# The state-space stage of a two-block transformer kernel: rotation and scan moved into PSUM, projections one block ahead

## Chip, cores and metric

One core of a Trainium2 chip runs the whole program in one launch. The metric is the device time of the execution in microseconds, as the median of several runs; beside it stands one execution that the hardware profiler recorded.

## What is computed

512 tokens of width 1024 pass through a first block (SwiGLU, gated mixer, SwiGLU) and a second one of depth 2, whose second layer has a diagonal state-space mixer ("S5") in place of attention. Only that mixer is touched. In the reference, cut to what matters:

```python
def s5_mixer(h, a_re, a_im, log_dt, b_re, b_im, c_re, c_im, d_skip, w_glu):
    u = h.reshape(B, L, 64, 16)                  # 64 groups of 16 channels
    ...                                          # ab = exp(a * dt), bb = coef * b, complex
    bu_re = jnp.einsum('blgc,gpc->blgp', u, bb_re)
    bu_im = jnp.einsum('blgc,gpc->blgp', u, bb_im)
    _, _, x_re, x_im = lax.associative_scan(_complex_scan_op, (ar, ai, bu_re, bu_im), axis=1)
    y = einsum('blgp,gcp->blgc', x_re, c_re) - einsum('blgp,gcp->blgc', x_im, c_im)
    y = y.reshape(B, L, D) + d_skip * u.reshape(B, L, D)
    ga, gb = jnp.split(jax.nn.gelu(y) @ w_glu, 2, axis=-1)
    return ga * jax.nn.sigmoid(gb)
```

## The kernel before, in words

Activations lie channel-major: X is eight tiles of 128 channels by 512 tokens. Large products run as three passes over operands split into a high and a low half (`mm3`, L259 to L262; `gemm`, L264); `weight` (L239) loads 128 x 1024 weights on SyncE's queue into one of four `raw` buffers (L242) and splits them on ScalarE (L245) and VectorE (L246) into one of three pairs.

The stage `s5` (L1196) works on eight blocks k of 128 channels, that is eight groups each. Four successive tokens are folded together: an earlier part (`ssm_prep`) has written to DRAM, for each k, seven 128 x 512 tables: two input matrices, cos and sin of the rotation, two output matrices and the direct taps. `s5` loads them back as Rf (four tables) and Rb_ (three), L1200 to L1203, on ScalarE's DMA queue, four buffers each. With the folding a scan runs over 128 steps in each of four quarters q of a tile, and the complex recurrence is turned into a real decay `rho` between a rotation by c, s and one back.

Per block: `ahead` scales and shifts the input on VectorE (L1215) and reorders tokens on ScalarE (L1217). `gather` (L1223) brings the four token phases onto the partitions by 16 identity matmuls (L1227) of 32 output rows and copies the bank to U (L1231). `front` (L1238) projects: eight matmuls (L1247) into two banks, copied to SBUF by ScalarE (L1249). Then the rotation: six products and sums (L1255 to L1260) split between VectorE and GpSimd (`W` is VectorE for blocks 0 and 1, then GpSimd), eight scans of 128 columns (L1264), two clears (L1270, L1271) and six products and sums back (L1276 to L1281) into xr and xi, whose first column is zero so that a matmul sees the state before its step. `back` (L1284) forms the output with 48 matmuls of 32 output rows (L1292), applies GELU (L1297), splits high and low (L1299, L1300) and adds the block's share of the first two GLU products (L1305), which thus accumulate through the stage; the other 14 follow at L1318. The loop at L1307 keeps two blocks in flight between `front` and `back`.

Tiles and semaphores come from a framework that orders the instructions of each engine by program order and by a timeline that it simulates itself, so that the order on an engine can differ from that of the text; each engine then works through its list in order. The PSUM pools `pa` and `pb` have four banks each.

Of the kernel before, what the change touches and what calls it, by code (L numbers as in the profile page):

```python
# [11 lines left out]
F32 = mybir.dt.float32  # L12
# [7 lines left out]
P = 128  # L20
T = 512
# [151 lines left out]
def emit(nc, tc, A, out):  # L173
    es = ExitStack()
    with es:
# [10 lines left out]
        def nm(s):  # L186
            uid[0] += 1
            return f"{s}{uid[0]}"
# [1005 lines left out]
                yield  # L1194

        def s5(rho, acc, then):  # L1196
            with tc.tile_pool(name="sg", bufs=3, reuse_waits="tile") as sg:
                RR = []
                for k in range(KT):
                    Rf = sg.tile([P, 4, T], F32, name=nm("R"), tag="Rf", bufs=4)  # L1200
                    S.dma_start(Rf, spill[k][:, :4])
                    Rb_ = sg.tile([P, 3, T], F32, name=nm("R"), tag="Rb", bufs=4)
                    S.dma_start(Rb_, spill[k][:, 4:])  # L1203
                    RR.append((Rf, Rb_))
                Rb = spread(norm(acc.parts()))
                g, sh = GS["m", 1]
                U = [xt() for _ in range(KT)]
                hs = []

                def ahead():  # L1210
                    k = len(hs)
                    if k == KT:
                        return
                    t = tt()
                    V.scalar_tensor_tensor(t, X[k], g[:, k : k + 1], Rb, op0=ALU.mult, op1=ALU.mult)  # L1215
                    h = xt()
                    S.activation(  # L1217
                        h.rearrange("p (s j) -> p s j", s=4), t.rearrange("p (j s) -> p s j", s=4), AF.Identity,
                        bias=sh[:, k : k + 1],
                    )  # L1220
                    hs.append(h)

                def gather(k):  # L1223
                    p = psb()
                    for q in range(4):
                        for s in range(4):
                            E.matmul(  # L1227
                                p[32 * s : 32 * s + 32, q * P : (q + 1) * P], ident[:, 32 * q : 32 * q + 32],
                                hs[k][:, s * P : (s + 1) * P], start=True, stop=True, tile_position=(0, 32 * s),
                            )  # L1230
                    S.activation(U[k], p, AF.Copy)  # L1231

                GH, GL = [], []
                early = [[weight(A["glu"][j]), psa()] for j in range(2)]

                ahead()

                def front(k):  # L1238
                    gather(k)
                    ahead()  # L1240
                    R = RR[k][0]
                    z = []
                    for j in range(2):
                        p = psb()
                        for q in range(4):
                            sl = slice(q * P, (q + 1) * P)
                            E.matmul(p[:, sl], R[:, j, sl], U[k][:, sl], start=True, stop=True)  # L1247
                        t = sg.tile([P, T], F32, name=nm("z"), tag=f"z{j}")
                        S.activation(t, p, AF.Copy)  # L1249
                        z.append(t)  # L1250
                    c, s = R[:, 2, :], R[:, 3, :]
                    W = V if k < 2 else G
                    a = sg.tile([P, T], F32, name=nm("z"), tag="za")
                    b = sg.tile([P, T], F32, name=nm("z"), tag="zb")
                    V.tensor_tensor(a, z[0], c, op=ALU.mult)  # L1255
                    W.tensor_tensor(b, z[1], s, op=ALU.mult)
                    V.tensor_tensor(a, a, b, op=ALU.add)
                    (G if k < 2 else V).tensor_tensor(z[1], z[1], c, op=ALU.mult)
                    G.tensor_tensor(z[0], z[0], s, op=ALU.mult)
                    W.tensor_tensor(b, z[1], z[0], op=ALU.subtract)  # L1260
                    for t in (a, b):
                        for q in range(4):
                            sl = slice(q * P, (q + 1) * P)
                            V.tensor_tensor_scan(  # L1264
                                t[:, sl], rho[:, 4 * k + q : 4 * k + q + 1].to_broadcast([P, P]), t[:, sl], 0.0,
                                op0=ALU.mult, op1=ALU.add,
                            )
                    xr = sg.tile([P, 4, 129], F32, name=nm("xr"), tag="xr")
                    xi = sg.tile([P, 4, 129], F32, name=nm("xi"), tag="xi")
                    G.memset(xr[:, :, 0:1], 0.0)  # L1270
                    G.memset(xi[:, :, 0:1], 0.0)  # L1271

                    def v4(t):
                        return t.rearrange("p (q j) -> p q j", j=P)

                    V.tensor_tensor(z[0], a, c, op=ALU.mult)  # L1276
                    W.tensor_tensor(z[1], b, s, op=ALU.mult)
                    V.tensor_tensor(xr[:, :, 1:], v4(z[0]), v4(z[1]), op=ALU.subtract)
                    G.tensor_tensor(a, a, s, op=ALU.mult)
                    V.tensor_tensor(b, b, c, op=ALU.mult)  # L1280
                    V.tensor_tensor(xi[:, :, 1:], v4(a), v4(b), op=ALU.add)  # L1281
                    return xr, xi

                def back(k, xr, xi):  # L1284
                    R = RR[k][1]
                    p = psb()
                    for i in range(4):
                        for j in range(3):
                            for q in range(4):
                                sl = slice(q * P + 32 * i, q * P + 32 * i + 32)  # L1290
                                rhs = (xr[:, q, :P], xi[:, q, :P], U[k][:, q * P : (q + 1) * P])[j]
                                E.matmul(  # L1292
                                    p[32 * q : 32 * q + 32, i * P : (i + 1) * P], R[:, j, sl], rhs,
                                    start=j == 0, stop=j == 2, tile_position=(0, 32 * q),
                                )
                    g = tt()
                    S.activation(g, p, AF.Gelu_apprx_tanh)  # L1297
                    h, l = xt(F32R), xt(F32R)
                    S.activation(h, g, AF.Copy)  # L1299
                    V.tensor_tensor(l, g, h.bitcast(F32), op=ALU.subtract)  # L1300
                    GH.append(h)
                    GL.append(l)
                    for w, p in early:
                        sl = slice(k * P, (k + 1) * P)
                        mm3(p, w[0][:, sl], w[1][:, sl], h, l, k == 0, k == KT - 1)  # L1305

                pend = []  # L1307
                for k in range(KT):
                    pend.append((k, *front(k)))
                    if len(pend) > 2:  # L1310
                        back(*pend.pop(0))
                while pend:
                    back(*pend.pop(0))
# [42 lines left out]
```

## Time and profile before

| | |
|---|---|
| Median of 3 runs | 2458.42 us (2456.69 to 2462.13) |
| The profiled execution's own time | 2460.43 us |
| Its span, first to last instruction | 2458.3 us |
| Mean granted TensorE clock | 0.974 of full speed |
| Busy: TensorE, VectorE, ScalarE, GpSimd | 95%, 60%, 36%, 25% |

The span is what the rows below divide up; the time of an execution is 2.1 us longer here. Engine names in rows: PE is TensorE (PEld its weight loads), DVE VectorE, ACT ScalarE, POOL GpSimd, SP SyncE; a q behind a name is the engine's sequencer. "L1264" is the line of the kernel, `out<-in` the program's tile names, and brackets at a row's end tell how long the engine had stood idle and what released it. An fp32 matmul is two instructions. The ends of matmuls are modelled, so distances between starts are the safer reading.

### The profile page before, as it was taken

What the parts mean: (1) busy time and instruction counts of PE and PEld (TensorE: products, weight loads), DVE (VectorE), ACT (ScalarE), POOL (GpSimd) and SP (SyncE); (2) the same over time, 40 slices, a digit from 0 to 9 for tenths busy, and PEclk for the clock granted to TensorE, in tenths of its full rate; (3) what the DMA queues carried; (4) which work ended last, traced back from release to release, by engine and by line L of the source; (5) the groups of instructions that cost most, each with busy time, mean ns of one, the idle gap of its engine ahead of it and who ended that gap; (6) DMA issues with size and microseconds to landing.
All of it is one profiled execution on the core that took longest, in us unless ns stands there. A gap on an engine that the chain in (4) does not pass through costs nothing.

```text
span 2458.3 us, 31106 instructions
## 1 busy us (share of the span) xinstructions
PE 2338.8 (95%) x11608; PEld 1895.4 (77%) x11608; DVE 1478.2 (60%) x2748; ACT 876.1 (36%) x1374; POOL 611.5 (25%) x821
## 2 busy tenths in 40 slices
PE   8999999999999999999999989999898679999999
PEld 6888888877888888887676578787687567888887
DVE  7555565455675555446996559777644964544443
ACT  3222233533333222234345634434333222433332
POOL 2212022240122121132001313656212530111211
PEclk9999999999999999999999999999998889999999
DMA  5444445323444444331121023343425312233332
GB/s 192 157 146 154 155 137 166 106 86 114 158 156 140 155 147 154 98 101 60 52 69 61 10 86 107 97 157 129 147 91 199 121 43 95 77 95 102 95 92 79
DMA packets 94087, 281.93 MB, mean 115 GB/s; under 512 B 9841, under 2 KB 14833, under 8 KB 91889
## 3 DMA queue, kind: packets, MB, share of 16 engines
q1 hardware_dynamic: 89184, 263.30, 33.2%
q10 hardware_dynamic: 4752, 16.65, 1.9%
q8 instruction: 91, 1.49, 0.2%
q14 instruction: 60, 0.48, 0.1%
HBM read 263.14 MB, written 16.78 MB: 114 GB/s over the span
## 4 chain that ended last, share of the span: by engine, by line
PE 79%; DVE 10%; POOL 4%; issue 3%; DMA 2%; ACT 2%; SPq 0%; ACTq 0%; DVEq 0%; POOLq 0%
PE pa L260 25%; PE pa L261 24%; PE pa L262 24%; DVE wl L246 1%; DVE z L1264 1%; PE pb L950 1%; DMA raw<-in_ada 1%; PE pb L939 1%; PE pa L905 1%; ACT wh L245 1%; PE pb L314 1%; PE pb L905 1%; PE pb L319 0%; PE pa L557 0%; POOL res L1041 0%
## 5 line engine op out<-in xcount | busy, mean ns | idle before, releaser
L261 PE MATMUL pa<-x,wh 128*128 128x512 f32 x1736 | 683.8, 394 | 18.3 <-DVE x L1300 13.8
L260 PE MATMUL pa<-x,wh 128*128 128x512 f32 x1736 | 680.2, 394 | 19.4 <-ACT x L343 7.8
L245 ACT ACTIVATE wh<-raw 128x1024 fp32r<-128x1024 f32 (+2 forms) x380 | 391.9, 1035 | 836.2 <-PE pa L261 656.7
L262 PE MATMUL pa<-x,wl 128*128 128x512 f32 x1736 | 680.7, 392 | 3.2 <-DVE wl L246 3.2
L246 DVE TENSOR_TENSOR wl<-raw,wh 128x1024 fp32r<-128x1024 f32 (+2 forms) x380 | 521.9, 1376 | 249.3 <-ACT wh L245 243.5
L260 PEld LDWEIGHTS pa<-x,wh 128*128 128x128 f32 x1736 | 328.4, 190 | 93.6 <-ACT x L1299 8.2
L261 PEld LDWEIGHTS pa<-x,wh 128*128 128x128 f32 x1736 | 328.8, 189 | 93.0 <-DVE x L1300 15.8
L262 PEld LDWEIGHTS pa<-x,wl 128*128 128x128 f32 x1736 | 329.0, 190 | 72.7 <-DVE wl L246 5.1
L260 PE MATMUL pa<-u,wh 128*128 128x512 f32 x704 | 276.2, 396 | 7.1 <-ACT u L1016 7.1
L261 PE MATMUL pa<-u,wh 128*128 128x512 f32 x704 | 276.8, 394 | 1.1 <-POOL u L1017 1.1
L262 PE MATMUL pa<-u,wl 128*128 128x512 f32 x704 | 275.0, 394 | 2.4 <-DVE wl L246 2.4
L368 DVE SCALAR_TENSOR_TENSOR ada<-raw,c,ada 128x512 f32<-128x512 f32 x168 | 129.5, 771 | 220.2 <-DMA raw<-in_ada 219.1
L402 POOL TENSOR_TENSOR t<-t,t 128x512 f32<-128x512 f32 x44 | 72.3, 1643 | 496.2 <-DVE t L401 286.5
L1013 POOL TENSOR_TENSOR t<-t,t 128x512 f32<-128x512 f32 x44 | 58.8, 1336 | 429.5 <-ACT t L1012 423.0
L260 PE MATMUL pa<-wh,x 128*128 128x512 f32 (+1 forms) x384 | 151.1, 401 | 14.4 <-DVE t L805 6.1
L260 PEld LDWEIGHTS pa<-u,wh 128*128 128x128 f32 x704 | 133.2, 189 | 39.2 <-ACT u L1016 8.4
L262 PEld LDWEIGHTS pa<-u,wl 128*128 128x128 f32 x704 | 133.6, 190 | 32.6 <-DVE wl L246 4.1
L261 PEld LDWEIGHTS pa<-u,wh 128*128 128x128 f32 x704 | 133.9, 190 | 30.5 <-POOL u L1017 1.9
L262 PE MATMUL pa<-wh,x 128*128 128x512 f32 (+1 forms) x384 | 150.6, 394 | 0.0
L261 PE MATMUL pa<-wl,x 128*128 128x512 f32 (+1 forms) x384 | 149.7, 390 | 0.0
L288 POOL TENSOR_TENSOR acc<-acc,t 128x512 f32<-128x512 f32 x45 | 73.0, 1628 | 174.2 <-ACT t L282 164.1
L260 PEld LDWEIGHTS pa<-wh,x 128*128 128x128 f32 x384 | 85.2, 223 | 31.9 <-issue 10.4
(360 smaller groups left out, 2885.6 us busy)
## 6 DMA issues: line engine op xcount, KB each, us to landing
raw<-in_ada SPq DMA_DIRECT2D x96, 512.0 KB, 3.9
raw<-in_u SPq DMA_DIRECT2D x88, 512.0 KB, 3.6
raw<-in_f1u SPq DMA_DIRECT2D x44, 512.0 KB, 3.7
raw<-in_f2u SPq DMA_DIRECT2D x44, 512.0 KB, 3.5
raw<-in_d SPq DMA_DIRECT2D x32, 512.0 KB, 3.5
raw<-in_aq SPq DMA_DIRECT2D x28, 512.0 KB, 3.8
dr<-res SPq DMA_DIRECT2D x8, 1536.0 KB, 7.6
raw<-in_wpg SPq DMA_DIRECT2D x20, 512.0 KB, 3.6
```

Of the source, the lines that this page charges most:

```text
L245: S.activation(h[:, :w], r[:, :w], AF.Copy)
L246: eng.tensor_tensor(l[:, :w], r[:, :w], h[:, :w].bitcast(F32), op=ALU.subtract)
L260: E.matmul(ps, ah, bh, start=first, stop=False)
L261: E.matmul(ps, ah, bl, start=False, stop=False)
L262: E.matmul(ps, al, bh, start=False, stop=last)
L288: G.tensor_tensor(self.sums[0], self.sums[0], sq, op=ALU.add)
L314: E.matmul(p[:, 8 * j + o + b : 8 * j + o + b + 1], a[:, tokens(b, by4)], ones, start=True, stop=True)
L368: V.scalar_tensor_tensor(acc, r[:, j * T : (j + 1) * T], kk, acc, op0=ALU.mult, op1=ALU.add)
L402: G.tensor_tensor(b, a, b, op=ALU.mult)
L905: E.matmul(ps[e][:, :W], QT[pr][base : base + 64, n * P : (n + 1) * P], KTT[pr][base : base + 64, :W], start=True, stop=True,)
L939: E.transpose(p[:, j * P : (j + 1) * P], s[:, j * P : (j + 1) * P], ident)
L1013: G.tensor_tensor(b, a, b, op=ALU.mult)
```

## The change

All of it lies in `s5`. What it does:

- The scaled input of blocks 1 to 7 is formed on GpSimd from an SBUF copy of the norm's factors; block 0 reads them from PSUM on VectorE. The gain moves into ScalarE's reordering instruction.
- The gather writes into the first of the block's two projection banks; the projection then overwrites that bank.
- `project` runs one block ahead of `front`: gather, copy to u, projection of the imaginary part first. It also has ScalarE spread rho over 512 columns (`rt`, column 0 of each quarter zero), so that one scan of 512 columns restarts at each quarter.
- The products, sums and scans of the rotation are done by VectorE in place in the two banks. For the way back ScalarE copies one part to SBUF and VectorE and GpSimd share the work; the last block has VectorE alone.
- xr, xi and rt live in fixed buffers, used alternately, whose zero columns are cleared once.
- The output product is 12 full-width matmuls over one bank; GELU follows, and a second gather (`blocks`) brings the result into channel order.
- One block rather than two is kept in flight; R of blocks 3 to 7 is loaded on SyncE's queue, Rb_ has three buffers.

The new text of the changed functions (what they replace is printed above):

```diff
...
                 for k in range(KT):
+                    q = S if k < 3 else nc.sync
                     Rf = sg.tile([P, 4, T], F32, name=nm("R"), tag="Rf", bufs=4)
+                    q.dma_start(Rf, spill[k][:, :4])
+                    Rb_ = sg.tile([P, 3, T], F32, name=nm("R"), tag="Rb", bufs=3)
+                    q.dma_start(Rb_, spill[k][:, 4:])
...
+                for t in (*xri, *rt):
+                    G.memset(t[:, :, 0:1], 0.0)
+                rp = spread(norm(acc.parts()))
+                Rb = kept(rp)
...
+                def blocks(p, src):
                     for q in range(4):
                         for s in range(4):
                             E.matmul(
                                 p[32 * s : 32 * s + 32, q * P : (q + 1) * P], ident[:, 32 * q : 32 * q + 32],
+                                src[:, s * P : (s + 1) * P], start=True, stop=True, tile_position=(0, 32 * s),
                             )
+                    return p
+
+                def ahead():
...
+                    if k == 0:
+                        V.tensor_tensor(t, X[k], rp, op=ALU.mult)
+                    else:
+                        G.tensor_tensor(t, X[k], Rb, op=ALU.mult)
+                    h = tt()
+                    S.activation(
+                        h.rearrange("p (s j) -> p s j", s=4), t.rearrange("p (j s) -> p s j", s=4), AF.Identity,
+                        bias=sh[:, k : k + 1], scale=g[:, k : k + 1],
+                    )
...
+                def project():
...
                     ahead()
+                    z = [psb(), psb()]
+                    u = sg.tile([P, T], F32, name=nm("U"), tag="U", bufs=4)
+                    S.activation(u, blocks(z[0], H[k]), AF.Copy)
...
+                    for j in (1, 0):
                         for q in range(4):
                             sl = slice(q * P, (q + 1) * P)
+                            E.matmul(z[j][:, sl], R[:, j, sl], u[:, sl], start=True, stop=True)
+                    S.activation(
+                        rt[k % 2][:, :, 1:], rho[:, 4 * k : 4 * k + 4].unsqueeze(2).to_broadcast([P, 4, 127]), AF.Copy
+                    )
...
+                def front(k):
+                    project()
+                    zr, zi = pre[k]
...
+                    d, a = st("z"), st("z")
+                    V.tensor_tensor(d, zi, c, op=ALU.mult)
+                    V.tensor_tensor(zi, zi, s, op=ALU.mult)
+                    V.tensor_tensor(a, zr, c, op=ALU.mult)
+                    V.tensor_tensor(zi, zi, a, op=ALU.add)
+                    V.tensor_tensor(zr, zr, s, op=ALU.mult)
+                    V.tensor_tensor(zr, d, zr, op=ALU.subtract)
+                    rk = rt[k % 2].rearrange("p q j -> p (q j)")
+                    for t in (zr, zi):
+                        V.tensor_tensor_scan(t, rk, t, 0.0, op0=ALU.mult, op1=ALU.add)
+                    wr, wi = zi, zr
...
+                    if k < KT - 1:
+                        S.activation(m[1], wi, AF.Copy)
+                        V.tensor_tensor(m[0], wr, c, op=ALU.mult)
+                        V.tensor_tensor(m[2], wr, s, op=ALU.mult)
+                        G.tensor_tensor(m[3], m[1], c, op=ALU.mult)
+                        G.tensor_tensor(xi[:, :, 1:], v4(m[2]), v4(m[3]), op=ALU.add)
+                        G.tensor_tensor(m[1], m[1], s, op=ALU.mult)
+                        G.tensor_tensor(xr[:, :, 1:], v4(m[0]), v4(m[1]), op=ALU.subtract)
+                    else:
...
+                def back(k, xr, xi):
+                    R = RR[k][1]
+                    p = psa()
+                    for j in (2, 1, 0):
                         for q in range(4):
                             sl = slice(q * P, (q + 1) * P)
+                            rhs = (xr[:, q, :P], xi[:, q, :P], U[k][:, sl])[j]
+                            E.matmul(p[:, sl], R[:, j, sl], rhs, start=j == 2 and q == 0, stop=j == 0 and q == 3)
+                    y = tt()
+                    S.activation(y, p, AF.Gelu_apprx_tanh)
+                    p = blocks(psa(), y)
                     h, l = xt(F32R), xt(F32R)
+                    S.activation(h, p, AF.Copy)
+                    V.tensor_tensor(l, p, h.bitcast(F32), op=ALU.subtract)
...
                     pend.append((k, *front(k)))
-                    if len(pend) > 2:
+                    if len(pend) > 1:
                         back(*pend.pop(0))
```

## Rows read from the trace of the kernel before

**Rows 1.** The page, part 1: busy time, share of the span, instructions.
```profile
PE 2338.8 (95%) x11608; PEld 1895.4 (77%) x11608; DVE 1478.2 (60%) x2748; ACT 876.1 (36%) x1374; POOL 611.5 (25%) x821
```

**Rows 2.** Busy time by stretch; columns: us, engines' busy us (instructions), clock, DMA.
```profile
1883.31:1898.44 15.13, 9.73 (x77) 8.83 (x77) 6.66 (x19) 5.02 (x6) 0.00 (x0) 0.57 0.99 394
1898.44:1952.03 53.59, 35.01 (x535) 29.52 (x534) 48.31 (x72) 16.47 (x24) 30.27 (x22) 0.80 0.43 153
1952.03:1965.22 13.19, 10.38 (x165) 8.36 (x164) 12.95 (x18) 4.80 (x8) 7.47 (x7) 1.00 0.32 107
```

**Rows 3.** Timeline of VectorE, one block; columns: start, duration, engine, line, operation.
```profile
1965.22 3.66 DVE L1264 TENSOR_TENSOR_SCAN z<-c,z 128x128 f32<-128x128 f32 x8
...
1971.07 1.77 DVE L1278 TENSOR_TENSOR xr<-z,z 128x512 f32<-128x512 f32 x1
1972.76 1.75 DVE L1280 TENSOR_TENSOR z<-z,R 128x512 f32<-128x512 f32 x1
...
1976.04 1.80 DVE L1257 TENSOR_TENSOR z<-z,z 128x512 f32<-128x512 f32 x1
...
1978.37 3.66 DVE L1264 TENSOR_TENSOR_SCAN z<-c,z 128x128 f32<-128x128 f32 x8
```

**Rows 4.** Timeline of GpSimd in that block.
```profile
1970.56 1.73 POOL L1279 TENSOR_TENSOR z<-z,R 128x512 f32<-128x512 f32 x1
1972.44 1.52 POOL L1256 TENSOR_TENSOR z<-z,R 128x512 f32<-128x512 f32 x1 [0.16 <-ACT z L1249]
```

**Rows 5.** Timeline of VectorE elsewhere, first operand in PSUM.
```profile
1143.33 0.68 DVE L804 TENSOR_TENSOR t<-pa,sm 128x512 f32<-128x512 f32 x1
1143.93 0.68 DVE L805 TENSOR_TENSOR t<-pa,sm 128x512 f32<-128x512 f32 x1
```

**Rows 6.** Timeline of all engines elsewhere: VectorE from PSUM beside GpSimd.
```profile
38.12 0.68 DVE L399 TENSOR_TENSOR t<-pa,rb 128x512 f32<-128x512 f32 x1
...
38.35 1.29 POOL L402 TENSOR_TENSOR t<-t,t 128x512 f32<-128x512 f32 x1 [16.97 <-ACT t L400]
```

**Rows 7.** Timeline of VectorE in block 0: an add, its four scans, what follows.
```profile
1904.04 0.66 DVE L1260 TENSOR_TENSOR z<-z,z 128x512 f32<-128x512 f32 x1
1904.74 1.37 DVE L1264 TENSOR_TENSOR_SCAN z<-c,z 128x128 f32<-128x128 f32 x4
1906.03 0.67 DVE L1276 TENSOR_TENSOR z<-z,R 128x512 f32<-128x512 f32 x1
```

**Rows 8.** VectorE groups by line and shape: busy us, mean ns.
```profile
L956 DVE TENSOR_TENSOR x<-pb,x 128x128 fp32r<-128x128 f32 x16 | 4.5, 281 | 10.8 <-ACT x L955 10.7
```

**Rows 9.** Timeline of TensorE, first blocks; x counts merged instructions.
```profile
1895.69 3.63 PE L1247 MATMUL pb<-x,R 128*128 128x128 f32 x16 [0.72 <-ACT x L1231]
...
1903.03 1.08 PE L1227 MATMUL pb<-x,c 128*32 128x128 f32 x32
1904.83 2.05 PE L1247 MATMUL pb<-x,R 128*128 128x128 f32 x16 [0.72 <-ACT x L1231]
...
1909.76 1.96 PE L1227 MATMUL pb<-x,c 128*32 128x128 f32 x32
```

**Rows 10.** Timeline of TensorE at the stage's end.
```profile
2008.33 0.95 PE L260 MATMUL pa<-x,wh 128*128 128x512 f32 x3 [0.71 <-ACT x L1299]
...
2009.39 0.40 PE L262 MATMUL pa<-x,wl 128*128 128x512 f32 x1
...
2010.31 0.39 PE L262 MATMUL pa<-x,wl 128*128 128x512 f32 x1
```

**Rows 11.** Timeline of ScalarE; ACTq is its queue issuing a DMA.
```profile
1891.78 1.21 ACT L1217 ACTIVATE x<-t,c 128x512 f32<-128x512 f32 x1 [6.96 <-DVE t L1215]
...
1912.43 0.60 ACT L1249 ACTIVATE z<-pb 128x512 f32<-128x512 f32 x1 [5.81 <-POOL z L1279]
```

**Rows 12.** Waits on SyncE's queue: who for whom, us, times, longest.
```profile
SPq L242 <- DVE wl L246: 98.6, 2, 94.8
```

**Rows 13.** DMA issues in the stage: count, KB each, us to landing.
```profile
R<-dr ACTq DMA_DIRECT2D x8, 1024.0 KB, 5.4
```

More of the change, by code (lines that the diff above doesn't have):

```diff
@@ L1233, in s5 @@
                 GH, GL = [], []
                 early = [[weight(A["glu"][j]), psa()] for j in range(2)]
-                ahead()
-                def front(k):
-                    gather(k)
+                pre = []
+                def project():
+                    k = len(U)
+                    if k == KT:
+                        return
                     ahead()
+                    z = [psb(), psb()]
+                    u = sg.tile([P, T], F32, name=nm("U"), tag="U", bufs=4)
+                    S.activation(u, blocks(z[0], H[k]), AF.Copy)
+                    U.append(u)
@@ L1251, in front @@
-                    c, s = R[:, 2, :], R[:, 3, :]
[L1252 to L1279, printed above, removed]
@@ L1280, in front, with v4 @@
-                    V.tensor_tensor(b, b, c, op=ALU.mult)
-                    V.tensor_tensor(xi[:, :, 1:], v4(a), v4(b), op=ALU.add)
+                            E.matmul(z[j][:, sl], R[:, j, sl], u[:, sl], start=True, stop=True)
+                    S.activation(
+                        rt[k % 2][:, :, 1:], rho[:, 4 * k : 4 * k + 4].unsqueeze(2).to_broadcast([P, 4, 127]), AF.Copy
+                    )
+                    pre.append(z)
+                ahead()
+                project()
+                def v4(t):
+                    return t.rearrange("p (q j) -> p q j", j=P)
@@ new lines, in front, with st @@
+                def front(k):
+                    project()
+                    zr, zi = pre[k]
+                    R = RR[k][0]
+                    c, s = R[:, 2, :], R[:, 3, :]
+                    def st(n):
+                        return sg.tile([P, T], F32, name=nm("z"), tag=n, bufs=3 if n == "z" else 2)
+                    d, a = st("z"), st("z")
[9 more added lines that the diff above has]
+                    wr, wi = zi, zr
+                    xr, xi = xri[2 * (k % 2)], xri[2 * (k % 2) + 1]
+                    m = [st(f"m{j}") for j in range(4)]
+                    if k < KT - 1:
[7 more added lines that the diff above has]
+                    else:
+                        V.tensor_tensor(m[3], wi, c, op=ALU.mult)
+                        V.tensor_tensor(m[1], wi, s, op=ALU.mult)
+                        V.tensor_tensor(wi, wr, s, op=ALU.mult)
+                        V.tensor_tensor(xi[:, :, 1:], v4(wi), v4(m[3]), op=ALU.add)
+                        V.tensor_tensor(wr, wr, c, op=ALU.mult)
+                        V.tensor_tensor(xr[:, :, 1:], v4(wr), v4(m[1]), op=ALU.subtract)
@@ L1285, in back @@
                     R = RR[k][1]
[L1286 to L1297, printed above, removed]
+                    p = psa()
+                    for j in (2, 1, 0):
+                        for q in range(4):
+                            sl = slice(q * P, (q + 1) * P)
+                            rhs = (xr[:, q, :P], xi[:, q, :P], U[k][:, sl])[j]
[3 more added lines that the diff above has]
+                    p = blocks(psa(), y)
                     h, l = xt(F32R), xt(F32R)
-                    S.activation(h, g, AF.Copy)
-                    V.tensor_tensor(l, g, h.bitcast(F32), op=ALU.subtract)
+                    S.activation(h, p, AF.Copy)
+                    V.tensor_tensor(l, p, h.bitcast(F32), op=ALU.subtract)
                     GH.append(h)
```

39 lines of the change are left out of this document (9 added, 30 removed).

## The prediction, made before the changed kernel was run

> **What bounds the kernel now.** I read the page's part 1 first: TensorE is busy for 95% of the span [rows 1], so over the whole kernel little can move. Its table of slices shows the exceptions, and the state-space stage is the longest of them, so I cut the span by stretch. From the last down-projection (1883.31 us) the stage has 15.1 us of start, in which TensorE has work for 9.7 us and the granted clock averages 0.57. From the first rotation product (1898.44) on, VectorE is busy 48.3 of 53.6 us, and later 12.95 of 13.19 us in one whole block of 128 channels, at clock 1.00 and with TensorE busy 10.4 us by modelled ends [rows 2]. Here VectorE sets the pace, not TensorE. The end of the stage is the last matmul of the two early GLU accumulations, 2010.31 + 0.39 = 2010.70 us [rows 10]; behind it TensorE is full again.
>
> VectorE's timeline of one block says why a block takes 13.15 us (the distance between the two rows of scans): eight scans take 3.6 us, and three two-operand instructions last 1.75 to 1.80 us [rows 3] where the same kind lasts 0.66 or 0.67 alone [rows 7]. GpSimd is reading SBUF in those moments [rows 4]. So some 3.3 us of the block are VectorE held while GpSimd runs, and one more is in the scans: four of them alone take 1906.03 - 1904.74 = 1.29 us, 0.32 each, or 2.6 for eight [rows 7].
>
> **The change part by part.**
>
> *Rotation and scan in PSUM.* The two copies of z by ScalarE go, and VectorE works in place on the projection's banks: six products and sums, two scans, then two products out (the last block: six), and the subtraction that splits off the low half, which now also reads PSUM. That is nine 512-column instructions and two scans per block; GpSimd keeps five. A VectorE instruction with one operand in PSUM starts every 0.60 us and lasts 0.68 [rows 5], no more than one fed from SBUF [rows 7]. And one that ran beside GpSimd kept its 0.68 us while GpSimd kept 1.29 [rows 6]. All of VectorE's steady work in the new stage has at most one operand in SBUF, so I take the holding of [rows 3] as gone. Nine by 0.60 is 5.4 us.
> [...]
> No row shows VectorE writing PSUM. Below 0.60 it cannot go, since the reading end alone sets that start distance; above, I bound it by each of the six writers taking its stream twice: four more 0.60 and two more scans, 4.6 us per block. I take 0.60, since rows 5 is the nearest, and keep the other end as a rival.
>
> *512-column scans.* No row has one. A scan of 128 columns lasts about 0.39 us (1.37 less three distances of 0.32 is 0.41, [rows 7]), a product of 128 columns 0.281 [rows 8] and one of 512 columns 0.68, so 384 columns more cost 0.40 at the product's rate, and 0.80 at twice that. From 0.32 that is 0.72 to 1.12 us each. The scan's extra 0.11 to 0.13 us at 128 columns fits the doubled rate (0.13 by the same slope), so I take 1.12, 2.24 for both. A dependent instruction starts about 0.70 after its source rather than 0.60 [rows 7]; four such places add 0.4.
> VectorE per block: 5.4 + 2.24 + 0.4 = 8.0 us (7.2 with the cheap scan), against 13.15.
>
> *Gather in the projection's bank, block-diagonal output at full width, second gather.* Per block TensorE issues a gather (32 instructions, 1.08 us), the projection (16 in 2.05) [rows 9], the output product as 12 full-width matmuls, 24 instructions, 3.1 us at the projection's pace, in place of 96 narrow ones, a second gather, 1.08, and six early matmuls at 0.23, 1.4 [rows 10]: 8.7 us. At the half clock, by the other rows of the same lines (1.96 and 3.63 us [rows 9]), it is 1.96 + 3.63 + 5.4 + 1.96 + 2.8 = 15.8. So TensorE comes level with VectorE and is late next. Its queue is in order, and three results come back through ScalarE in each block: the gathered u, the GELU and the high half. One such wait is 0.72 us [rows 9]; if none is filled with other work, 8.7 + 2.2 = 10.9 us per block.
>
> *Input scaling moved to GpSimd (blocks 1 to 7).* GpSimd: five instructions by 1.29 [rows 6], 6.5 us, under both. The 128-row zero columns are cleared once rather than per block; they cost nothing on a GpSimd with this slack. If the slack went, 0.1 us each.
>
> *ScalarE.* Out: two z copies. In: one m copy, one decay table, a u copy and GELU and high half as before. 1.21 + five by 0.60 [rows 11] is 4.2 us, 4.8 if the broadcast table costs as much as the strided 1.21. Hidden under 8 us. The Rb copy of the norm lies beside the first scaled input, which now reads the bank itself.
>
> *Loads of R for blocks 3 to 7 moved to SyncE's queue.* On ScalarE's queue a load that waited for its buffer held ScalarE for 5.81 us [rows 11]; that goes. On SyncE's queue they stand among the GLU weight loads, one of which waited 94.8 us for a buffer [rows 12]. Ten loads, each behind its own freed buffer: a 1 MB load lands 5.4 us after issue [rows 13], against a block of 8 to 9 us and a projection a block ahead, so I cost it at nothing; with three rather than four Rb buffers the load of block k+3 waits for the output product of block k, and Rf of the next stands behind it. If that cover failed, each block would wait up to 5.4 us.
>
> *One block less in flight, projections a block ahead.* The z banks come in pairs of four, so projection k+2 waits for rotation k. It then needs 1.08 + 0.72 + 2.05 = 3.9 us, and rotation k+1 lasts 8, which covers it.
>
> **The sum.** Rotation 0 can begin when the first half of the projection is done, 1895.69 + 1.8 = 1897.5 us [rows 9]. Two blocks without an output product at 8.0, six at 9.5 (between VectorE's 8.0 and TensorE's unfilled 10.9) make 73 us. The last block has four more products on VectorE, 2.4. Behind them: last eight matmul instructions 1.0, GELU 0.7, gather 1.1, high half 0.7, low half 0.7, last early matmuls 0.9, so 5.1, and 2 for a part of it at half clock. 1897.5 + 73 + 2.4 + 5.1 + 2 = 1980.0 against 2010.7: 30.7 us saved. The profiled execution took 2460.43 us with a span of 2458.3, 2.0 above the median of the runs; 2460.4 - 30.7 = 2429.7, and from the median 2458.4, **2427.7 us**. About 0.2% (5 us) is what a measurement of this kernel can tell from no change.
>
> **The rivals.**
> - *VectorE alone sets the pace.* With TensorE's waits all filled a block takes 7.2 to 8.0 us. Eight blocks are 58 to 64, and 9 to 15 us more are saved than in the sum: 2412 to 2419 us. For it: the order before already slips gathers between output products (1903.03, with no idle time shown [rows 9]). Against it: 8.7 us of TensorE work per block. Chance 0.15.
> - *Writing PSUM costs a second stream*, or waits pile up. A block takes up to 8.0 + 4.6 = 12.6 us; eight are 101, and about 3 us are saved at the far end, 2455 us; halfway 2441. No row speaks against it; rows 5 speak for the reading end alone. Chance 0.15, a fifth of it within 0.2%.
> - *The holding stays.* If products fed from PSUM are also held by GpSimd, five GpSimd instructions hold VectorE 1.1 us each and a block takes 13.5: no change, 2458 us. Rows 6 speak against it. Chance 0.03.
> - *Slower: TensorE at half clock.* The place is blocks 1 to 7: each hand-over leaves TensorE idle, the clock falls, and the 15.8 us of a block then exceed the 13.15 it has now. From 1893.7 us (the first projection less its gather, [rows 9]) eight blocks by 15.8 and a tail of 7, the 5.1 with its TensorE part doubled, end near 2027, 16 us late: 2475. It decides once more than about two thirds of a block's TensorE work runs at half clock (8.7 to 15.8 passes 13.15). For it: clock 0.57 at the start and 0.80 in the next stretch [rows 2]. Against it: 1.00 in a block whose pace VectorE set, so with more idle time for TensorE than the new one leaves [rows 2]. [...] Chance 0.07.
>
> **How the numbers follow.** The forecast itself, 8.0 to 10.9 us per block in steady state, has 0.60: from 2418 (six blocks 1.5 faster) to 2437. Faster takes forecast, the first rival and four fifths of the second: 0.87 and a little of the half-clock case where it holds only part of the stage, 0.89. Within 0.2%: the held case and a fifth of the second, 0.05. Slower 0.06. The range drops the ends of the first rival and the last two: 2414 to 2446.
>
> **What would show each step.** Right: VectorE's products at 0.68 us with GpSimd busy beside them, GpSimd at 1.26 to 1.29 throughout, scans near 1.2 us, rotations 8 to 10 us apart, the last early matmul near 1980. Wrong: in-place products above 0.8 us (second rival); products of 1.7 us (the holding); projection rows of 3.6 us in blocks 3 to 7 with clock near 0.5 (half clock); VectorE waiting for TensorE more than 2 us a block (TensorE's waits dearer than 10.9); TensorE's projection waiting for a DMA (SyncE's queue).

## The result, and the profile after

| | before | after |
|---|---|---|
| Median, on the same chip | 2460.28 us | 2430.38 us (2426.51 to 2431.24) |
| Ratio | 1 | 0.9877 [0.9861, 0.9894] |
| The profiled execution's own time | 2460.43 us | 2431.24 us |
| Its span | 2458.3 us | 2429.5 us |

(A fourth execution took 4470.66 us, for a reason not looked into; it is in the median of the right column but not in the ratio or the bounds.) The change makes the kernel 1.2% faster, 2.7 us above the forecast of 2427.7 and inside its range. The first part of the page, to be read beside [rows 1], follows; line numbers from here on are those of the changed kernel.

```profile
PE 2338.0 (96%) x11288; PEld 1900.8 (78%) x11288; DVE 1449.9 (60%) x2701; ACT 875.9 (36%) x1374; POOL 599.4 (25%) x810
```

To see the stage alone I measure it between two instructions that every version has: VectorE's first step on the norm's statistics (L334) and its first weight split behind the stage (L246), in "stage" below. Before it ran from 1886.35 to 2010.68 us, 124.3; after from 1888.65 to 1981.42, 92.8. So 31.6 us went out of it. Of that 2.3 are missing in the span because the stage begins later in this execution (its start lay between 1880.9 and 1888.7 us over the versions below, whose code ahead of the stage is the same; what sets it was not tried), and 0.5 behind it: 31.6 - 2.3 - 0.5 = 28.8.

VectorE's timeline of one block, during which GpSimd worked without a gap (beside [rows 3]):

```profile
1923.36 0.69 DVE L1279 TENSOR_TENSOR z<-pb,R 128x512 f32<-128x512 f32 x1
1923.96 0.69 DVE L1280 TENSOR_TENSOR pb<-pb,R 128x512 f32<-128x512 f32 x1
1924.56 0.68 DVE L1281 TENSOR_TENSOR z<-pb,R 128x512 f32<-128x512 f32 x1
1925.16 0.69 DVE L1283 TENSOR_TENSOR pb<-pb,R 128x512 f32<-128x512 f32 x1
1925.76 0.69 DVE L1282 TENSOR_TENSOR pb<-pb,z 128x512 f32<-128x512 f32 x1
1926.36 0.69 DVE L1284 TENSOR_TENSOR pb<-z,pb 128x512 f32<-128x512 f32 x1
1926.95 2.33 DVE L1287 TENSOR_TENSOR_SCAN pb<-rt,pb 128x512 f32<-128x512 f32 x2
1929.19 0.67 DVE L1293 TENSOR_TENSOR z<-pb,R 128x512 f32<-128x512 f32 x1
1929.78 0.67 DVE L1294 TENSOR_TENSOR z<-pb,R 128x512 f32<-128x512 f32 x1
1930.38 0.68 DVE L1279 TENSOR_TENSOR z<-pb,R 128x512 f32<-128x512 f32 x1
```

GpSimd's timeline in it (beside [rows 4]):

```profile
1925.31 1.28 POOL L1296 TENSOR_TENSOR xri<-z,z 128x512 f32<-128x512 f32 x1
1926.54 1.28 POOL L1297 TENSOR_TENSOR z<-z,R 128x512 f32<-128x512 f32 x1
1927.78 1.27 POOL L1232 TENSOR_TENSOR t<-x,rb 128x512 f32<-128x512 f32 x1
```

Every product and sum on VectorE, those that write PSUM in place too, lasts 0.67 to 0.69 us, and the next instruction starts 0.60 us after it; GpSimd keeps 1.28. Two scans take 1929.19 - 1926.95 = 2.24 us. This block lasts 7.02 us; with the subtraction of a low half, which falls between blocks here, 7.6, against 13.15 before.

Busy time by stretch (columns as in [rows 2]), cut at the first products of blocks 0, 3, 4, 5, 6 and 7, at block 7's way back and at the stage's end:

```profile
1886.00:1900.97 14.97, 8.64 (x74) 7.74 (x74) 4.61 (x16) 8.62 (x10) 3.88 (x5) 0.67 1.01 413
1900.97:1923.36 22.39, 18.02 (x212) 15.67 (x212) 21.84 (x32) 8.75 (x13) 10.61 (x9) 0.84 0.40 144
1923.36:1930.38 7.02, 7.02 (x96) 6.41 (x98) 7.02 (x11) 2.20 (x4) 7.02 (x7) 1.00 0.47 168
1930.38:1941.98 11.60, 11.60 (x150) 9.94 (x141) 8.37 (x13) 5.73 (x9) 10.31 (x9) 1.00 0.75 292
1941.98:1950.23 8.25, 8.25 (x115) 7.67 (x114) 7.72 (x12) 4.01 (x6) 3.13 (x3) 1.00 0.29 97
1950.23:1959.00 8.77, 8.16 (x110) 7.13 (x110) 7.75 (x12) 2.67 (x5) 6.17 (x6) 1.00 0.27 92
1959.00:1966.32 7.32, 7.32 (x86) 6.29 (x88) 6.63 (x9) 1.19 (x2) 3.00 (x3) 1.00 0.01 2
1966.32:1981.43 15.11, 13.40 (x120) 10.66 (x112) 5.07 (x9) 2.89 (x5) 0.00 (x0) 1.00 0.00 1
```

VectorE sets the pace up to 1923 (21.84 of 22.39 us). From block 3 on TensorE has nearly no gap (one of 0.6 us up to 1959), while VectorE has some after its full block 3: blocks 3 to 6 take 1959.00 - 1923.36 = 35.64 us, 8.9 each, where VectorE needs 7.6. Its waits, from the groups by line (1898 to 1985 us; busy, mean ns, then idle time before them by releaser):

```profile
L1279 DVE TENSOR_TENSOR z<-pb,R 128x512 f32<-128x512 f32 x8 | 5.5, 685 | 8.5 <-PE pb L1257 8.4
L1281 DVE TENSOR_TENSOR z<-pb,R 128x512 f32<-128x512 f32 x8 | 5.5, 682 | 1.6 <-PE pb L1257 1.6
L1321 DVE TENSOR_TENSOR x<-pa,x 128x512 fp32r<-128x512 f32 x8 | 5.5, 682 | 6.6 <-ACT x L1320 6.6
```

Most of this lies at the two ends: 6.4 us of L1279's wait stand ahead of block 0, and 4.4 of L1321's in the tail. Within blocks 3 to 6 VectorE waits 4.8 us in all, 2.5 for the projection and 2.3 for a high half.

### The profile page after: what moved, and what is told of

Its sections match the earlier page's. It is cut to its first block, busy times and chain, and to the rows that moved or that the text cites. A ratio compares the mean times of both kernels' runs of the same rounds, so it can differ in the third digit from the quotient of the medians.

```text
span 2429.5 us, 30407 instructions
## 1 busy us (share of the span) xinstructions
PE 2338.0 (96%) x11288; PEld 1900.8 (78%) x11288; DVE 1449.9 (60%) x2701; ACT 875.9 (36%) x1374; POOL 599.4 (25%) x810
## 4 chain that ended last, share of the span: by engine, by line
PE 77%; DVE 10%; POOL 4%; issue 4%; DMA 3%; ACT 2%; ACTq 0%; SPq 0%; DVEq 0%; POOLq 0%
PE pa L260 24%; PE pa L262 23%; PE pa L261 23%; DMA raw<-in_ada 2%; DVE wl L246 2%; PE pb L950 1%; PE pb L314 1%; PE pb L939 1%; ACT wh L245 1%; DVE x L723 1%; PE pa L905 1%; PE pb L905 1%; PE pb L1257 1%; POOL t L1013 0%; POOL res L1041 0%
## 5 line engine op out<-in xcount | busy, mean ns | idle before, releaser
L246 DVE TENSOR_TENSOR wl<-raw,wh 128x1024 fp32r<-128x1024 f32 (+2 forms) x380 | 520.9, 1373 | 259.7 <-ACT wh L245 249.7
L262 PEld LDWEIGHTS pa<-u,wl 128*128 128x128 f32 x704 | 132.9, 189 | 31.4 <-DVE wl L246 3.0
L260 PEld LDWEIGHTS pa<-wh,x 128*128 128x128 f32 x384 | 85.5, 223 | 31.4 <-issue 10.4
```

The lines of the kernel that those rows point to most:

```text
L246: eng.tensor_tensor(l[:, :w], r[:, :w], h[:, :w].bitcast(F32), op=ALU.subtract)
L260: E.matmul(ps, ah, bh, start=first, stop=False)
L262: E.matmul(ps, al, bh, start=False, stop=last)
```

## The experiments

All ten work on the changed kernel. Diffs are against it; where a version builds on another experiment, the text says so.

| version | median us | ratio to before | stage us |
|---|---|---|---|
| before | 2458 to 2460 | 1 | 124.3 |
| changed | 2430.38 | 0.9877 [0.9861, 0.9894] | 92.8 |
| e_sbuf | 2459.5 | 1.0005 [0.9994, 1.0017] | 124.0 |
| e_vec | 2442.39 | 0.9936 [0.9919, 0.9953] | 108.0 |
| e_sbufvec | 2443.86 | 0.9943 [0.9928, 0.9958] | 110.4 |
| e_scan128 | 2431.03 | 0.9895 [0.9877, 0.9913] | 93.5 |
| e_dve2 | 2431.83 | 0.9901 [0.9884, 0.9917] | 98.2 |
| e_narrow | 2419.52 | 0.9853 [0.9836, 0.9871] | 86.4 |
| e_nargather | 2434.31 | 0.9902 [0.9886, 0.9919] | 96.5 |
| e_gelu | 2420.78 | 0.9842 [0.9828, 0.9857] | 85.8 |
| e_best2 | 2425.0 | 0.9862 [0.9846, 0.9877] | 89.3 |
| e_actq | 2427.86 | 0.9879 [0.9863, 0.9896] | 93.2 |

The ratios also carry the start of the stage, which shifts from one execution to the next; the stage column does not, but it is one execution each, so how far it scatters is not known.

**e_sbuf: rotation and scan in SBUF again.**

```diff
-                    zr, zi = pre[k]
+                    zs = []
+                    for j in range(2):
+                        t = xt()
+                        S.activation(t, pre[k][j], AF.Copy)
+                        zs.append(t)
+                    zr, zi = zs
```

> The changed kernel, but ScalarE copies both projection banks to SBUF and the rotation and the scans work there. Theory (a VectorE instruction with one operand in PSUM is not held while GpSimd reads): with both operands in SBUF again, products that meet a GpSimd instruction last 1.7 to 1.8 us instead of 0.68; some four or five of them per block add 4 to 5 us to VectorE's 7.5, a block goes from 8.9 to 11.5 to 13 us and the time to 2447 to 2460 us. Rival (the gain is from the 512-column scans, the projections ahead and one kind of output matmul): VectorE stays below TensorE's 8.9 us a block, the copies are hidden on ScalarE, 2430 us within 5.

The whole gain is gone: ratio 1.0005, stage 124.0 us, at the slow end of the theory's range. Groups by line of this kernel (1898 to 2000 us), three of VectorE and one of GpSimd:

```profile
L1284 DVE TENSOR_TENSOR z<-x,R 128x512 f32<-128x512 f32 x8 | 10.3, 1292 | 10.6 <-ACT x L1274 10.6
L1285 DVE TENSOR_TENSOR x<-x,R 128x512 f32<-128x512 f32 x8 | 9.8, 1221 | 0.0
L1326 DVE TENSOR_TENSOR x<-pa,x 128x512 fp32r<-128x512 f32 x7 | 4.8, 688 | 15.2 <-ACT x L1325 15.2
```

```profile
L1300 POOL TENSOR_TENSOR z<-z,R 128x512 f32<-128x512 f32 x7 | 14.8, 2111 | 44.1 <-ACT z L1297 44.1
```

The same products that last 685 and 690 ns from PSUM now average 1292 and 1221, and GpSimd is held in turn (2111 instead of 1280). L1326, the one with an operand in PSUM, keeps its 688. Over the six lines of products with R VectorE is busy 47.9 us against 31.4 in the changed kernel, 16.5 of the 31.2 us lost. But VectorE also waits for ScalarE, 25.8 us in the rows of L1284 and L1326 (9.2 of them ahead of block 0), and TensorE's mean granted clock from the first product of block 2 to that of block 6 is 0.87 against 0.96. So this run alone could not tell the holding, with what queues behind it, from the extra pass through ScalarE. The next two do.

**e_vec and e_sbufvec: the same pair without GpSimd.** e_vec puts GpSimd's five instructions of a block on VectorE, which also makes ScalarE's copy for the way back needless; e_sbufvec has in addition the copies of e_sbuf.

```diff
-                        G.tensor_tensor(t, X[k], Rb, op=ALU.mult)
+                        V.tensor_tensor(t, X[k], Rb, op=ALU.mult)
...
-                        S.activation(m[1], wi, AF.Copy)
-                        V.tensor_tensor(m[0], wr, c, op=ALU.mult)
-                        V.tensor_tensor(m[2], wr, s, op=ALU.mult)
-                        G.tensor_tensor(m[3], m[1], c, op=ALU.mult)
-                        G.tensor_tensor(xi[:, :, 1:], v4(m[2]), v4(m[3]), op=ALU.add)
-                        G.tensor_tensor(m[1], m[1], s, op=ALU.mult)
-                        G.tensor_tensor(xr[:, :, 1:], v4(m[0]), v4(m[1]), op=ALU.subtract)
+                        V.tensor_tensor(m[3], wi, c, op=ALU.mult)
+                        V.tensor_tensor(m[1], wi, s, op=ALU.mult)
+                        V.tensor_tensor(m[2], wr, s, op=ALU.mult)
+                        V.tensor_tensor(m[0], wr, c, op=ALU.mult)
+                        V.tensor_tensor(xi[:, :, 1:], v4(m[2]), v4(m[3]), op=ALU.add)
+                        V.tensor_tensor(xr[:, :, 1:], v4(m[0]), v4(m[1]), op=ALU.subtract)
```

> The changed kernel with all element-wise work of the stage on VectorE: GpSimd's scaled input and its four products and sums of the way back move there (five instructions by 0.60 us), the ScalarE copy in front of them goes. Everything else as changed, rotation in PSUM. VectorE's block grows from 7.2 to 10.2 us, past the 8.9 us that TensorE sets now, so about 1.3 us in each of seven blocks: near 2440 us (2436 to 2446). It is the control for the next kernel: no GpSimd work beside VectorE in either.

> The same, and in addition ScalarE copies both projection banks to SBUF and VectorE rotates and scans there, as in the SBUF experiment that lost the whole gain (2459.5 us). Theory A, the gain was lost because GpSimd holds VectorE when both read SBUF: without GpSimd work nothing holds it, products last 0.67 us, and it is as fast as its control, within 5 us (2440 to 2446), so faster than with GpSimd's help. Theory B, the gain was lost through the extra pass through ScalarE (two copies of 0.6 us between projection and rotation, and behind other ScalarE work): it stays 20 to 30 us behind its control, 2460 to 2470 us, with VectorE waiting for ScalarE for several us in each block.

2442.39 us, as expected, and 2443.86: with GpSimd out of the way, going back to SBUF costs 2.4 us of stage; with GpSimd at work it costs 31.2. The 2.4 us lie at the start: the first product comes 16.4 us after the statistics instead of 13.6, and between there and the tail VectorE never waits for ScalarE. Theory A holds, B falls (with the reservation that VectorE is full in both of these, so that the pair does not show what the longer way through ScalarE costs where VectorE has slack). The products in SBUF, groups by line of e_sbufvec, last what they last in PSUM, for which one line of e_vec follows:

```profile
L1285 DVE TENSOR_TENSOR x<-x,R 128x512 f32<-128x512 f32 x8 | 5.6, 699 | 0.0
L1284 DVE TENSOR_TENSOR z<-x,R 128x512 f32<-128x512 f32 x8 | 5.6, 697 | 8.3 <-ACT x L1274 8.3
```

```profile
L1280 DVE TENSOR_TENSOR pb<-pb,R 128x512 f32<-128x512 f32 x8 | 5.6, 696 | 0.0
```

So GpSimd's help is worth 15 us of stage with the rotation in PSUM (108.0 to 92.8), and costs 14 with it in SBUF (110.4 to 124.0). Both kinds of source stand side by side in e_sbuf: 1221 ns with two operands in SBUF (L1285), 688 with one in PSUM (L1326).

**e_scan128: eight 128-column scans in place of two of 512,** still in PSUM.

```diff
-                        V.tensor_tensor_scan(t, rk, t, 0.0, op0=ALU.mult, op1=ALU.add)
+                        for q in range(4):
+                            sl = slice(q * P, (q + 1) * P)
+                            V.tensor_tensor_scan(
+                                t[:, sl], rho[:, 4 * k + q : 4 * k + q + 1].to_broadcast([P, P]), t[:, sl], 0.0,
+                                op0=ALU.mult, op1=ALU.add,
+                            )
```

> The changed kernel with eight scans of 128 columns per block again, in PSUM, in place of two of 512. Theory (TensorE, busy without a gap from the fourth block on, sets the pace at 8.9 us a block, and the long scan only runs at the half rate that its 1.13 us shows): VectorE gets 8 x 0.32 - 2 x 1.13 = 0.3 us more per block and stays under TensorE: 2430 us within 4. Rival (the long scans are a main part of the gain): eight start-ups more on the path of each block, 1 us or more per block, 2438 us or more.

2431.03 us, stage 93.5: no difference that can be told. The long scans are no measurable part of the gain. The projections a block ahead and the smaller moves were not taken back one by one; e_sbuf, which keeps them, has no gain left.

**e_dve2: 1.2 us more VectorE work per block,** one product formed three times.

```diff
+                    V.tensor_tensor(a, zr, c, op=ALU.mult)
+                    V.tensor_tensor(a, zr, c, op=ALU.mult)
                     V.tensor_tensor(zi, zi, a, op=ALU.add)
```

> The changed kernel with one product per block (zr by c) done three times over: 1.2 us more on VectorE per block, 9.6 us in all, same result. Theory (TensorE is the bound from the fourth block on, VectorE in the first three and in the last): VectorE goes from 7.2-7.8 to 8.4-9.0 us, about level with TensorE's 8.9; 3 to 6 us slower, 2433 to 2436 us. Rival (VectorE still sets the pace in all blocks): the whole 9.6 us, 2440 us.

1.5 us in the median, 5.4 in the stage, of 9.6 us added; by the ratios it is 6 us, but their intervals overlap. The stage is as the theory had it, the median below its 3 to 6 us. The place tells which engine leads where. From L334 to the first product of block 3 it is 1924.85 - 1887.20 = 37.65 us against 34.71, 2.9 of the 3.6 us added there; from block 3 to block 7 it is 1962.25 - 1924.85 = 37.40 against 35.64, 1.8 of 4.8. So VectorE leads at first and later has slack: 3.0 of the 4.8 us vanish in four blocks, about 0.8 a block.

**e_narrow and e_nargather: TensorE's work.** e_narrow forms the output directly in channel order by narrow matmuls, u's part first, so that the second gather goes (1.06 to 1.08 us of TensorE per block). e_nargather, whose diff (the second) is against e_narrow, puts that gather back as dead work.

```diff
                     for j in (2, 1, 0):
-                        for q in range(4):
-                            sl = slice(q * P, (q + 1) * P)
-                            rhs = (xr[:, q, :P], xi[:, q, :P], U[k][:, sl])[j]
-                            E.matmul(p[:, sl], R[:, j, sl], rhs, start=j == 2 and q == 0, stop=j == 0 and q == 3)
+                        for i in range(4):
+                            for q in range(4):
+                                sl = slice(q * P + 32 * i, q * P + 32 * i + 32)
+                                rhs = (xr[:, q, :P], xi[:, q, :P], U[k][:, q * P : (q + 1) * P])[j]
+                                E.matmul(
+                                    p[32 * q : 32 * q + 32, i * P : (i + 1) * P], R[:, j, sl], rhs,
+                                    start=j == 2 and i == 0, stop=j == 0 and i == 3, tile_position=(0, 32 * q),
+                                )
                     y = tt()
                     S.activation(y, p, AF.Gelu_apprx_tanh)
-                    p = blocks(psa(), y)
                     h, l = xt(F32R), xt(F32R)
-                    S.activation(h, p, AF.Copy)
-                    V.tensor_tensor(l, p, h.bitcast(F32), op=ALU.subtract)
+                    S.activation(h, y, AF.Copy)
+                    V.tensor_tensor(l, y, h.bitcast(F32), op=ALU.subtract)
```

```diff
                     S.activation(y, p, AF.Gelu_apprx_tanh)
+                    blocks(psa(), y)
                     h, l = xt(F32R), xt(F32R)
```

> The changed kernel with the output product in 48 matmuls of 32 output rows again (U's part still first), which need no second gather. Theory (TensorE sets the pace from the fourth block on): a block has 96 narrow instructions, 2.6 us at full clock, in place of 24 wide ones and a gather, 4.1 us; TensorE falls from 8.7 to 7.2 us a block, VectorE's 7.5 to 8 takes over, the tail loses a gather and a wait: 5 to 10 us faster, 2420 to 2425 us. Rival (VectorE or the waits between the engines already set the pace): within 3 us of 2430, or slower by the narrow matmuls at half clock.

> The narrow-output experiment (2419.5 us; 86.4 us from the norm's statistics to the first weight split behind the stage, against 92.8 in the changed kernel) with the second gather put back as dead work: 32 narrow matmuls of the GELU's result into a PSUM bank that nobody reads, 1.08 us of TensorE per block. Theory A, the changed kernel is paced by TensorE's sum of work: TensorE has 7.5 us of work in a 7.6 us block of the narrow version, so 1.1 us more makes a block 8.6 us and gives back most of the gain: 91 to 94 us of stage, 2425 to 2429. Theory B, the chain through the second gather (gather, then high half, then early products) is what costs, not the work: the dead gather is filled in, and the stage stays within 2 us of 86.4, the time at 2418 to 2421.

e_narrow takes 6.4 us out of the stage, and its 2419.52 us lie just below the range of the theory. So the full-width output with its second gather is a part of the change that cost time. From block 3 to block 7 VectorE is now full in every block, 31.17 of 31.17 us; TensorE has no gap in the first two of these four and gaps of 0.15 and 0.92 us in the others (the third block, then the sum of the four, columns as above):

```profile
1938.33:1945.94 7.61, 7.46 (x150) 6.16 (x142) 7.61 (x13) 4.15 (x7) 6.84 (x6) 1.00 0.43 147
sum 31.17, PE 30.11 PEld 25.43 DVE 31.17 ACT 14.69 POOL 25.09; mean PE 7.53 PEld 6.36 DVE 7.79 ACT 3.67 POOL 6.27
```

The dead gather alone gives all of that back and 3.7 us more. (The ratios of e_narrow and of the changed kernel overlap, as do those of the changed kernel and e_nargather; the times themselves, each version on another chip, do not: 2419.03 to 2424.17 us, 2426.51 to 2431.24 without the 4470.66, and 2432.40 to 2437.64.) That its result is used by nobody excludes the chain behind it (theory B); its place behind the GELU in TensorE's list remains. The sum of work (A) has the direction but not the size, 10.1 us of stage where 8 x 1.08 = 8.6 were added. The timeline of e_nargather, all engines, shows one place where more than the work is lost:

```profile
1933.15 0.63 ACT L1324 ACTIVATE x<-t 128x512 fp32r<-128x512 f32 x1
...
1934.03 2.33 DVE L1287 TENSOR_TENSOR_SCAN pb<-rt,pb 128x512 f32<-128x512 f32 x2
...
1937.45 1.48 DVE L1325 TENSOR_TENSOR x<-t,x 128x512 fp32r<-128x512 f32 x1
...
1938.99 0.50 PE L261 MATMUL pa<-x,wh 128*128 128x512 f32 x1 [2.87 <-DVE x L1325]
...
1940.04 1.95 PE L1257 MATMUL pb<-U,R 128*128 128x128 f32 x16
...
1941.13 0.69 DVE L1279 TENSOR_TENSOR z<-pb,R 128x512 f32<-128x512 f32 x1 [2.20 <-PE pb L1257]
```

The high half is ready at 1933.78, but VectorE's list has scans and products ahead of the subtraction for the low half (L1325), which starts at 1937.45 and, with both inputs in SBUF and GpSimd at work beside it, lasts 1.48 us (672 ns on average in e_gelu below, with one input in PSUM). TensorE, in order, waits 2.87 us for it with the next projection (L1257) standing behind; and VectorE then waits 2.20 us for that projection. The same comes once more, ahead of block 7: TensorE waits 0.69 us for a low half at 1957.24, and VectorE 1.75 for the projection behind it at 1958.94. In e_narrow TensorE waits for a low half twice, 1.7 us in all, but VectorE for no projection after block 0's. So two lists in order, each waiting for the other, can cost more than the added work; how the 10.1 us divide was not tried.

**e_gelu and e_best2: two more edits on e_narrow.** e_gelu is e_narrow with GELU in place in PSUM (`y = p` for `y = tt()`), so that the low half reads one operand from PSUM. e_best2 has in addition the norm's copy behind block 0's scaled input.

```diff
-                Rb = kept(rp)
...
                 ahead()
+                Rb = kept(rp)
                 project()
```

> The narrow-output experiment with GELU in place in its PSUM bank alone (without moving the norm's copy): the low half's subtraction then has one operand in PSUM and always lasts 0.69 us. In the narrow version it was held twice, by 0.96 and 0.69 us. VectorE sets the pace there: 1 to 2 us less of stage, 84.5 to 85.5 us, 2417 to 2420. If the order of work shifts as in the version with both edits, 87 to 90 us of stage.

> The narrow-output experiment (2419.5 us) with two edits more: the copy of the norm's factors goes behind block 0's scaled input, which had waited for it (about 0.7 us at the start), and GELU writes in place to its PSUM bank, so that the subtraction for the low half has one operand in PSUM and isn't held by GpSimd (it lasted 1.4 to 1.6 us at times, up to 0.9 us in some of eight blocks). If VectorE sets the pace there, as its trace without gaps says, 2 to 6 us less: 2414 to 2418. If TensorE's order of work sets it after all, only the first 0.7 us: 2419.

e_gelu: the low half's mean falls from 886 to 672 ns, the stage from 86.4 to 85.8 us, less than the 1 to 2 us expected, and its ratio 0.9842 [0.9828, 0.9857] lies clear of the changed kernel's; against e_narrow's it can't be told apart. These two are the fastest measured. e_best2 missed: 2425.0 us, not 2414 to 2418 or 2419. The scaled input does start 0.6 us sooner after the statistics, but ScalarE's list then has another reordering ahead of the copy of u, as its timeline shows:

```profile
1896.37 1.30 ACT L1233 ACTIVATE t<-t,c,c 128x512 f32<-128x512 f32 x1 [1.39 <-POOL t L1231]
1897.57 0.58 ACT L1250 ACTIVATE U<-pb 128x512 f32<-128x512 f32 x1
```

The first rotation product comes 12.5 us after the statistics (1900.31 - 1887.78), in e_narrow 12.4, and VectorE waits for two later projections, 1.03 and 0.93 us. These are 2 of the 3.5 us of stage by which it lies behind e_gelu; the rest was not traced.

**e_actq: all loads of R on ScalarE's queue.**

```diff
-                    q = S if k < 3 else nc.sync
+                    q = S
```

> The changed kernel with all R loads on ScalarE's queue, as before the change. Theory: a load that waits for its buffer (the five loads of Rb waited 29 us for the output product on SyncE's queue) holds ScalarE, which now feeds TensorE three times a block; some of it shows, 2434 to 2445 us, with ScalarE idle several us behind TensorE or VectorE at the loads. Rival: the buffers come free before ScalarE gets there, so the queue makes no difference: within 3 us of the changed kernel's 2430.

2427.86 us, stage 93.2: the rival was right, the queue makes no difference.

## Why the prediction was right, and where its sum was off

**What bounds.** Right, as far as was tried: VectorE, held by GpSimd, set the pace before. The two pairs show, in the changed kernel, that the place in PSUM pays because it ends the holding: 31.2 - 2.4 = 29 us of stage, 16.5 of them in the products themselves and the rest in what queues behind, which the pairs do not divide. The kernel before was not run without GpSimd's share.

**The rotation in PSUM.** "I take 0.60" and "the holding of [rows 3] as gone" both held: nine instructions 0.60 us apart, 0.67 to 0.69 long, beside a GpSimd at 1.28. The bound of a second stream for writing PSUM (4.6 us a block) fell; its rival goes with it. A PSUM source cost no more than an SBUF one: the same six products and sums last 697 to 700 ns from SBUF in e_sbufvec and 690 to 701 from PSUM in e_vec.

**The scans.** 1.12 us each was what they take: 2.24 for two, where products of the same width start 0.60 apart.

**VectorE per block.** The sum said 8.0; it is 7.6. The step that failed is "four such places add 0.4": the order on VectorE has L1283 ahead of L1282, so that most instructions find their source done, and the rest are 0.60 apart too.

**TensorE comes level and is late next.** Right, from block 3 on; the first rival, VectorE alone, holds only up to there. The six blocks "at 9.5 (between VectorE's 8.0 and TensorE's unfilled 10.9)" were too dear, 8.9 in the four measured; the waits for ScalarE are filled by other work. From the first product to the last sum (1970.05 + 0.68) it took 69.8 us, where the sum had 73 + 2.4 = 75.4: 5.6 too many, 3.1 in blocks 0 to 2 (22.4 instead of 25.5), 2.4 in blocks 3 to 6.

**The start.** 1897.5 us was 3.5 too soon: 2.3 from where the stage begins in this execution, 1.2 inside. All engines' timeline shows the inner part:

```profile
1893.14 0.60 ACT L327 ACTIVATE rb<-pb 128x512 f32<-128x512 f32 x1 [3.25 <-PE pb L319]
...
1893.84 0.69 DVE L1230 TENSOR_TENSOR t<-x,pb 128x512 f32<-128x512 f32 x1 [2.86 <-ACT rb L327]
...
1898.85 3.36 PE L1257 MATMUL pb<-U,R 128*128 128x128 f32 x14 [0.95 <-ACT U L1251]
...
1900.97 0.69 DVE L1279 TENSOR_TENSOR z<-pb,R 128x512 f32<-128x512 f32 x1 [6.44 <-PE pb L1257]
```

"The Rb copy of the norm lies beside the first scaled input" was wrong: the scaled input came behind it, 0.7 us later. Another 0.3 us is that the first product came 2.1 us after the projection's start, not 1.8; what is left are small differences on the way. But e_best2 shows that taking the copy away does not by itself bring the 0.7 back.

**The tail.** 5.1 + 2 us was 3.6 too short; it took 1981.43 - 1970.73 = 10.7. The 2 us for half clock were not needed, at clock 1.00. What the sum left out stands in TensorE's timeline:

```profile
1973.31 1.08 PE L1218 MATMUL pa<-t,c 128*32 128x128 f32 x32 [0.75 <-ACT t L1317]
1974.32 0.50 PE L260 MATMUL pa<-x,wh 128*128 128x512 f32 x1
...
1979.22 0.84 PE L260 MATMUL pa<-x,wh 128*128 128x512 f32 x3
...
1981.04 0.39 PE L262 MATMUL pa<-x,wl 128*128 128x512 f32 x1
```

From 1974.32 to 1979.22 TensorE runs 21 matmuls of the third GLU product, and only then the last early ones. The kernel before has the same number of such matmuls ahead of this point (24 of each of the three lines in both stages), but ran most of them sooner: behind its last high half stand nine, six of them early ones [rows 10]. The three errors, 3.5 - 5.6 + 3.6 us, nearly cancel: 1981.4 instead of 1980.0. That the forecast came within 2.7 us is luck in this sense; its mechanism held, its terms were off by 3 to 6 us each.

**SyncE's queue.** Costed at nothing, and right: Rb's loads waited there for the output product (rows: who waits for whom; then the loads, us to landing), and no engine waited for a load of R. That the old queue "held ScalarE" was true, but in the changed kernel its release bought nothing measurable either (e_actq).

```profile
SPq L1204 <- PE pa L1315: 29.1, 5, 8.3
```

```profile
R<-dr SPq DMA_DIRECT2D x5, 1024.0 KB, 6.3
```

**The clock.** 0.67 at the start and 0.84 in the first blocks, then 1.00: the slower rival's half clock covered no more than the old kernel's did [rows 2]. By the rival's own point, two thirds of a block's work at half clock, it was far off from block 3 on: TensorE waited once, 0.6 us, between there and block 7, so the idling that the rival feared did not arise.

## What to carry to other kernels

Where VectorE and GpSimd share element-wise work, count VectorE's SBUF inputs: leaving one operand in PSUM, even in place, cost nothing here (690 to 701 ns against 697 to 700 from SBUF) and turned GpSimd's help from a loss of 14 us of stage into a gain of 15. Once two engines come level, their orders matter beside their sums (e_nargather lost 10.1 us of stage to 8.6 of work): look for the instruction that stands in an in-order list behind one that waits for the other engine. And price a stage between two instructions that both kernels have, with the later work that fills its gaps counted in, or that work comes back as a longer tail (10.7 us here, where 7.1 were summed).

## What the runs showed of the hardware that was not expected

The holding goes both ways, more strongly than the 1.52 and 1.73 us of [rows 4]: in e_sbuf, where VectorE's products have both inputs in SBUF, GpSimd's L1300 averaged 2111 ns instead of 1280, its other four instructions 1381 to 1526 instead of 1272 to 1283. VectorE's in-place products on PSUM, read and write in one bank, cost no more than a read from PSUM into SBUF (690 and 685 ns by group, 0.60 us apart).
